# Which PSUM banks share a tile in the scan's paired column blocks, and how the planner of the order sees PSUM

## The chip, the cores and the metric

The kernel runs on one core of a Trainium2 chip. The metric is the time of one launch on the device, in microseconds (us), lower is better. A core has engines that work side by side, each with a queue of instructions of its own that it takes in order: TensorE (PE, matrix products into PSUM), VectorE (DVE), ScalarE (ACT), GpSimd (POOL), and SyncE (SP), whose queue here issues the loads and stores (DMAs). Engines wait for each other through semaphores. Products land in PSUM, in banks of 512 fp32 columns; the kernel's tiles there take eight banks.

## The reference

One layer of a streaming encoder for 512 prompt tokens and 64 sample tokens, which the kernel treats together as T = 576 columns. A combined input projection feeds a sparse attention (branch A) and a Mamba-2 scan (branch B); both are merged, and a SwiGLU FFN follows. The change lies in branch B, which in the reference is:

```python
full = jnp.concatenate([state_conv, xbc], axis=1)
xbc_c = jax.nn.silu(causal_conv(full, w_conv, b_conv, t))
xs, bm, cm = jnp.split(xbc_c, [D_INNER, D_INNER + SSM_GROUPS * D_STATE], axis=-1)
...
y, h_last = ssd_scan(xh, dtp, -jnp.exp(a_log), bm, cm, state_ssm, min(SSD_CHUNK, t))
y = (y + d_skip[:, None] * xh).reshape(b, t, D_INNER) * jax.nn.silu(z)
y = rms_normalize(y.reshape(b, t, SSM_GROUPS, -1)).reshape(b, t, D_INNER) * g_ssm_norm
```

xbc is a part of h @ w_in. It has 32 blocks of 128 channels: for each of the eight groups g two blocks of x (2g, 2g+1), one of B (16+g) and one of C (24+g). Each block is projected, convolved over four taps, and put through SiLU; then the scan goes over the tokens in chunks of 128 (and one of 64 for the sample stream).

## The kernel before

**Products.** Everything is fp32, and each matrix is kept as a high part and a low part in the type fp32r (names ending in h and l: hTh, hTl for the activations, wh, wl for a weight's two parts). A product is the sum of three matmul passes: high by high, high by low, low by high. The T columns are cut in halves of TH = 288.

**Pairs.** For groups 2 to 6 (PAIRED) the two x blocks are made together with Strassen's scheme, from seven products in place of eight. Product p takes an operand from the activations (A11, A12, A22, or one of the sums S1 to S4, kept in shS and slS) and one from the weights. Each product is 12 matmuls of 128x288: four slices, three passes. pair_split prepares the seven weights in four steps, two at a time: the first of a step goes to a tile of tag wh, the second to one of tag wl, and here each of these tiles holds a weight's high and low part both. So in the profile products 1, 6, 5, 3 appear with wh and 7, 2, 4 with wl; 1, 2, 4 with hTh and hTl, and 7, 6, 5, 3 with shS and slS.

Three banks collect them (PAIR): x takes 1, 6, 5, 3 one upon the other, z takes 7 and 4, y takes 2. After each product its bank is evicted into xc, the input of the convolution: by ScalarE copies after 1, 7, 6 and 3, and by VectorE adds after 2, 5 and 4 (LANDS). A half that holds sample columns is evicted in two pieces, 224 and 64 wide. Then the bank goes on: the next product adds to what stands in it. stage_a(g, 2) issues products 1, 7, 6, 2, and stage_a(g, 3) issues 5, 4, 3 and the two convolutions (conv_out).

**PSUM tiles.** pmm makes a tile of two banks (tag mm, two slots taken in turn), px a tile of one (tags px and py, two slots each). pair_begin takes two tiles of tag mm: y is in the first bank of one, x and z are the two banks of the other. Groups 0, 1 and 7, and every B and C block, use fm instead: one mm tile, each half of the columns in a bank. So a paired group takes four mm slots: B, C, and the pair's two.

**The convolution** (conv_out) of one block is: a small copy of the state (cvo), ScalarE's u = w3 * xc + bias (cu), three VectorE steps that add the other taps (cu), ScalarE's tanh (cth), and two VectorE steps that form SiLU into xb.

**The scan.** stage_b(g, c) does chunk c of group g: decay matrices on POOL and ScalarE (dec), transposes of x and B by TensorE, weighted copies (xdt, xw, bt, cs), the state (hst), and the products of y. In the loop over g, stage_b(g, i) is followed by stage_a(g+1, i) for i = 0 to 3, so the projections of the next group fill TensorE while a group is scanned. Every second group stage_c normalises two groups.

**The planner.** build() doesn't emit instructions at once. Each call makes an Op in a Plan; order() then simulates the engines with estimated costs (cost) and picks, per engine, the ready operation with the lowest prio (the running number, less an offset: R.prio(4000) puts an operation ahead of 4000 earlier ones). emit() issues the operations in the planned order, all from one line, which is why every row of the profile says L545. What depends on what is found by _touch from the boxes of the views (View.box): for PSUM, box() gives the 512-wide banks that a view covers. The semaphores themselves aren't set by the planner: the layer below adds them, from the accesses to each tile in the order in which they are emitted.

**Weight splits.** fetch() loads weights in queue order and split() makes their two parts: ScalarE copies the high part; the low part is a VectorE subtraction, or, for queue items 27 to 47, a second ScalarE pass and an accumulating DMA issued by POOL. Items 27 and 28 are the last two blocks of the filler work behind the attention's first key head.

Of the kernel before, what the change touches and what calls it, by code (L numbers as in the profile page):

```python
# [13 lines left out]
P = 128  # L14
D = 1024
NP_, NS = 512, 64
T = NP_ + NS
TH = T // 2
# [14 lines left out]
class View:  # L33
# [91 lines left out]
    def box(self):  # L125
        b = self.base
        if b.kind == "psum":
            f0 = self.off % b.pitch
            last = f0 + sum((n - 1) * s for n, s in self.dims[1:])
            return (0, P, f0 // 512 * 512, last // 512 * 512 + 512)  # L130
        if b.kind == "dram":
            last = self.off + sum((n - 1) * s for n, s in self.dims)
            return (0, 1, self.off, last + 1)
        p0, f0 = divmod(self.off, b.pitch)
        last = f0 + sum((n - 1) * s for n, s in self.dims[1:])
        return (p0, p0 + self.dims[0][0], f0, last + 1)
# [113 lines left out]
class Plan:  # L250
# [92 lines left out]
    def cost(self, op, outs, ins):  # L343
        e, fn = op.eng, op.fn
        o = outs[0] if outs else None
        if e == "sync":
            v = o if o is not None else ins[0]
            n = 4
            for k in v.shape:
                n *= k  # L350
            op.bytes = n
            row = 4 * v.shape[-1]
            op.rate = 300e3 if row >= 4096 else 345e3 if row >= 1024 else 250e3 if row >= 512 else 225e3
            return 0.06, 0.93
        if fn == "dma_start" and e == "scalar":
            op.bytes = 4 * _cols(ins[0]) * ins[0].shape[0]
            return 0.45, 0.93
        n = _cols(o)
        if e == "tensor":
            op.mm = True  # L360
            if fn == "transpose":
                return 0.110, 0.10
            rhs = op.args[2]
            fast = rhs.dtype == F32R
            n = _cols(rhs)
            if fast:
                return (n / 2.25 + 4 if n > 128 else 110) / 1e3, 0.10
            if op.kw.get("tile_position") is not None:
                return (73 if o.shape[0] <= 32 else 132) / 1e3, 0.10
            return ((4 * max(n, 128) / 2.4 if n > 1 else 190) + 5) / 1e3, 0.10  # L370
        if fn == "dma_start":
            op.bytes = 4 * n * o.shape[0]
            return 0.9, 0.93
        psum = any(is_psum(v) for v in ins)
        if e == "scalar":
            t = n / 1.2 + (52 if psum else 92) + (96 if isinstance(op.kw.get("bias"), View) else 0)
            return (t + (93 if op.kw.get("accum_out") is not None else 0)) / 1e3, 0.19
        if e == "vector":
            if fn == "tensor_reduce":
                n = _cols(ins[0])  # L380
            if fn in ("max", "match_replace"):
                n = _cols(ins[0] if fn == "max" else o)
            if fn == "reciprocal":
                return (69 + 6.25 * n) / 1e3, 0.13
            src = sum(1 for v in ins if _cols(v) > 1)
            fast = src == 1 and fn in ("tensor_copy", "tensor_scalar") and not is_psum(o) and not psum
            column = fn in ("scalar_tensor_tensor", "tensor_scalar") and len(ins) > src
            more = 60 * column + 70 * (fn == "tensor_tensor_reduce")
            return (64 + 0.96 * more + n * (0.5 if fast else 1.0)) / 0.96e3, 0.13
        if fn == "memset":  # L390
            return (n * 0.5 + 60) / 1e3, 0.1
        if op.kw.get("op") == OP.pow or OP.pow in op.args:
            return (n * 165 + 300) / 1e3, 0.1
        per = {"tensor_copy": 3.33, "affine_select": 1.0, "tensor_tensor": 2.1}[fn]
        return (n * per + 150) / 1e3, 0.1
# [157 lines left out]
def build(tc, I, O):  # L553
    R = Plan(tc)
# [3 lines left out]
    psum = R.mkpool("ps", space=PSUM)  # L558
# [5 lines left out]
    def pmm(name):  # L564
        return psum.tile([P, 2, 512], F32, name=name, tag="mm", bufs=2)
# [23 lines left out]
    def load_raw(src, nk, n):  # L589
        raw = wp.tile([P, nk, n], F32, name=f"raw{cnt[0]}", tag="raw", bufs=NRAW)  # L590
        sync.dma_start(raw, src)
        return raw
# [25 lines left out]
    raws, outs, outs_made = {}, {}, []  # L618
# [51 lines left out]
    def fetch(done, limit=1 << 30):  # L670

        while len(outs_made) < len(specs):
            i = len(outs_made)
            outs_made.append(i)
            queue.extend((i, s) for s in specs[i])
            outs[i] = []
        with R.prio(4000 if done else 0):
            more = True
            while more:
                more = False  # L680
                j = state["ld"]
                need = 0
                if j < min(len(queue), limit):
                    need = 1 if queue[j][1][0] != "pair" else 0 if queue[j][1][3] else 2
                if j < min(len(queue), limit) and raw_open[0] + need <= NRAW and j < state["sp"] + 4:
                    i, s = queue[j]
                    raw_open[0] += need
                    if s[0] == "pair":
                        w, c0 = s[1:3]
                        if need:  # L690
                            g, u = (load_raw(kview(w[:, c0 + P * a:c0 + P * a + P]), 8, P) for a in range(2))
                            pair_raw[c0] = {"B11": g[:, 0:4], "B21": g[:, 4:8], "B12": u[:, 0:4], "B22": u[:, 4:8]}
                        raws[j] = (c0, s[3])
                    elif s == "misc":
                        raw = wp.tile([P, 8, 104], F32, name="rawm", tag="raw", bufs=NRAW)
                        sync.dma_start(raw[:, :, 0:72], kview(w_in[:, C_KI:C_KI + 72]))
                        sync.dma_start(raw[:, :, 72:104], kview(w_in[:, C_DT:C_DT + 32]))
                        raws[j] = (raw, 8, 104)
                    else:
                        raws[j] = (load_raw(*s), s[1], s[2], 27 <= j < 48)  # L700
                    state["ld"] += 1
                    more = True
                j = state["sp"]
                if j < min(state["ld"], limit) and (j < NWH or queue[j - NWH][0] < done):
                    if queue[j][1][0] == "pair":
                        raw_open[0] -= 2 * (queue[j][1][3] == 3)
                        outs[queue[j][0]].append(pair_split(*raws.pop(j)))
                    else:
                        raw_open[0] -= 1
                        outs[queue[j][0]].append(split(*raws.pop(j)))  # L710
                    state["sp"] += 1
                    more = True
# [66 lines left out]
    for tb in range(5):  # L779
        n = P if tb < 4 else NS  # L780
        t = sp.tile([P, D], F32, name=f"xt{tb}")
# [125 lines left out]
    for tb in range(5):  # L907
        n = P if tb < 4 else NS
# [56 lines left out]
    with R.prio(-1500):  # L965
        for tb in range(5):
            n = P if tb < 4 else NS
# [23 lines left out]
    t = px("pwc")  # L991
# [76 lines left out]
    for i in range(2):  # L1068
        g = gqk[:, i, :]
# [120 lines left out]
    for hf in range(2):  # L1190
        x = ap_.tile([P, 5, 256], F32, name=f"qi{hf}", tag="tok", bufs=2)
# [69 lines left out]
    for b in range(5):  # L1261
        n = P * (b + 1) if b < 4 else T
# [3 lines left out]
    for b in (4, 1, 2, 3):  # L1266
        smp = b == 4
        n = T if smp else P * (b + 1)
# [200 lines left out]
    pair_now = {}  # L1469

    def pair_begin(g):
        py_, pxz = pmm(f"px{g}y"), pmm(f"px{g}x")
        pair_now[g] = {"y": py_[:, 0, :TH], "x": pxz[:, 0, :TH], "z": pxz[:, 1, :TH],
                       "xc": [conv_in(f"cv{g}_{i}", 2 * g + i - 2) for i in (2, 3)]}

    def pair_product(g, p):
# [137 lines left out]
    def stage_a(g, i):  # L1614
        if i == 0:
            bcs[g] = sd.tile([P, 2, T + 3], F32, name=f"bcx{g}", tag="bcx", bufs=3)
        if i == 2:

            xbs[g] = sd.tile([P, 2 * T + P - NS], F32, name=f"xb{g}", tag="xb", bufs=3)
            pool.memset(xbs[g][:, 2 * T:], 0.0)  # L1620
        if i >= 2 and g in PAIRED:
            if i == 2:
                pair_begin(g)
            for p in ((1, 7, 6, 2), (5, 4, 3))[i - 2]:
                pair_product(g, p)
            if i == 3:
                for a in range(2):
                    conv_out(f"cv{g}_{2 + a}", 2 * g + a, pair_now[g]["xc"][a], xbs[g][:, a * T:(a + 1) * T])
                del pair_now[g]
            return  # L1630
        ft = (16 + g, 24 + g, 2 * g, 2 * g + 1)[i]
        dst = bcs[g][:, i, :] if i < 2 else xbs[g][:, (i - 2) * T:(i - 1) * T]
        conv(f"cv{g}_{i}", ft, fm(f"px{g}_{i}", getw(), hh, hl), dst)
# [796 lines left out]
```

## Time and profile before

| what | value |
|---|---|
| time, three runs | 1382.48 us median (1381.15 to 1383.5) |
| the profiled execution: its time | 1381.79 us |
| the profiled execution: its span | 1380.1 us |
| granted TensorE clock, mean | 0.998 |
| instructions | 27974 |
| ScalarE copies xc<-mm in the whole kernel | 96, 207 to 413 ns |
| VectorE adds xc<-xc,mm in the whole kernel | 20, 208 to 456 ns |
| VectorE convolution steps cu | 96, median 817 ns |

The span reaches from the first to the last instruction of one execution; the time of that execution is a little longer. A row of the timeline has start, duration, engine, line, operation, output<-inputs, shapes, a count, and in brackets how long the engine stood idle before it and which engine and tile ended that. The durations of matmuls overlap: each is listed with about 0.29 us, while the next of a stream starts 0.13 to 0.14 us after it. PEld is the weight load that goes with a matmul. A view of waits has waiting engine and tile, releasing engine and tile, then total us, times, and the longest. A view of groups has busy time and mean ns of one, then the idle time ahead of them and who ended it. Names are the program's with numbers left out: xc is any group's convolution input, mm any tile of that tag.

### The profile page before, as it was taken

The page shows a single profiled execution, that of the slowest core. Times are in us where ns is not written, and L with a number is a line of the kernel's source. Part 1 is how long each engine was busy: PE and PEld are TensorE (multiplying, and loading weights), DVE is VectorE, ACT ScalarE, POOL GpSimd, SP SyncE. Part 2 cuts the span into 40 slices and gives each one's busy share as a digit, 9 for nine tenths or more (in the row PEclk, how much of TensorE's full clock was granted, in tenths as well). Part 3 has the DMA queues.
Part 4 walks back from the last instruction along what each step waited for, and adds up shares of the span by engine and source line. Part 5 has one row for each costly group of instructions (what it writes and reads, how often), then busy time and mean ns, then how long its engine had stood idle before and what let it go on. Part 6 is the DMA issues. An engine that isn't in the chain of part 4 may idle for free.

```text
span 1380.1 us, 27974 instructions
## 1 busy us (share of the span) xinstructions
PE 1344.9 (97%) x10617; PEld 1301.1 (94%) x10617; DVE 1168.2 (85%) x2354; ACT 818.0 (59%) x1873; POOL 200.4 (15%) x254
## 2 busy tenths in 40 slices
PE   7999999999999999989999999999999999999998
PEld 6999999999999888888889999999999999999998
DVE  5788999786778798888889769887799999888897
ACT  5435344777776677867878553124576666666453
POOL 2212003230300111322323320001100000000000
PEclk9999999999999999999999999999999999999999
DMA  9772436573853434333475578778623343325352
GB/s 300 218 191 68 118 111 160 115 177 95 193 150 88 121 94 112 101 111 97 134 214 148 196 231 272 239 213 251 187 63 108 93 130 100 92 71 156 96 158 65
DMA packets 268454, 201.36 MB, mean 146 GB/s; under 512 B 25552, under 2 KB 239680, under 8 KB 268320
## 3 DMA queue, kind: packets, MB, share of 16 engines
q1 hardware_dynamic: 263056, 183.40, 45.2%
q0 software_dynamic: 4976, 16.05, 5.9%
q8 instruction: 83, 1.36, 0.4%
q14 instruction: 51, 0.42, 0.1%
q10 hardware_dynamic: 288, 0.13, 0.0%
HBM read 157.75 MB, written 28.96 MB: 135 GB/s over the span
## 4 chain that ended last, share of the span: by engine, by line
PE 78%; ACT 8%; DVE 5%; DMA 4%; issue 3%; POOL 1%; SPq 0%; DVEq 0%; POOLq 0%; ACTq 0%
PE mm L545 54%; PE py L545 14%; PE px L545 10%; DMA raw<-in_w_in 2%; DVE cu L545 1%; ACT wh L545 1%; DVE wl L545 1%; ACT dec L545 1%; ACT hst L545 1%; ACT xc L545 1%; ACT cu L545 1%; ACT wl L545 1%; DMA y_d<-xb 1%; POOL r L545 0%; DVE wh L545 0%
## 5 line engine op out<-in xcount | busy, mean ns | idle before, releaser
L545 ACT ACTIVATE wh<-raw 128x1024 fp32r<-128x1024 f32 (+3 forms) x144 | 136.2, 948 | 138.3 <-PE mm L545 95.1
L545 PE MATMUL mm<-hTh,wl 128*128 128x288 f32 (+1 forms) x944 | 214.4, 303 | 2.6 <-ACT xc L545 1.9
L545 PE MATMUL mm<-hTh,wh 128*128 128x288 f32 (+1 forms) x904 | 205.0, 302 | 0.6 <-ACT wh L545 0.5
L545 PE MATMUL mm<-hTl,wh 128*128 128x288 f32 (+1 forms) x884 | 200.5, 302 | 0.9 <-DVE hTl L545 0.9
L545 PEld LDWEIGHTS mm<-hTh,wl 128*128 128x128 f32 (+1 forms) x944 | 154.1, 189 | 5.4 <-ACT xc L545 2.6
L545 PEld LDWEIGHTS mm<-hTh,wh 128*128 128x128 f32 (+1 forms) x904 | 147.6, 189 | 3.2 <-ACT hTh L545 0.8
L545 PEld LDWEIGHTS mm<-hTl,wh 128*128 128x128 f32 (+1 forms) x884 | 144.8, 189 | 3.2 <-DVE hTl L545 1.4
L545 DVE TENSOR_TENSOR wl<-raw,wh 128x1024 fp32r<-128x1024 f32 (+2 forms) x89 | 110.9, 1249 | 13.9 <-ACT wh L545 13.5
L545 POOL DMA_DIRECT2D wl<-raw x24 | 21.3, 889 | 468.6 <-PE px L545 313.8
L545 DVE SCALAR_TENSOR_TENSOR cu<-xc,wc,cu 128x579 f32<-128x579 f32 x96 | 80.0, 846 | 0.6 <-ACT cu L545 0.4
L545 PE MATMUL mm<-wh,hTl 128*128 128x256 f32 x256 | 72.5, 284 | 0.0
L545 PE MATMUL mm<-wl,hTh 128*128 128x256 f32 x256 | 72.3, 283 | 0.0
L545 PE MATMUL mm<-wh,hTh 128*128 128x256 f32 x256 | 72.2, 284 | 0.0
L545 DVE SCALAR_TENSOR_TENSOR aacc<-adr,sil,aacc 128x512 f32<-128x512 f32 x84 | 58.4, 748 | 6.3 <-DMA adr<-in_w_ada 6.2
L545 PE MATMUL mm<-shS,wh 128*128 128x288 f32 x248 | 55.0, 308 | 3.8 <-ACT xc L545 2.2
L545 PE MATMUL mm<-yh,wl 128*128 128x288 f32 x256 | 55.1, 296 | 0.0
L545 PE MATMUL mm<-xhS,wh 128*128 128x290 f32 (+1 forms) x248 | 54.8, 296 | 0.0
L545 PE MATMUL mm<-yh,wh 128*128 128x288 f32 x256 | 54.6, 295 | 0.0
L545 PE MATMUL mm<-yl,wh 128*128 128x288 f32 x256 | 54.6, 294 | 0.0
L545 ACT ACTIVATE P<-lg,mn 128x128 f32<-128x128 f32 (+4 forms) x72 | 41.7, 581 | 19.2 <-DVE mn L545 18.3
L545 PE MATMUL mm<-xhS,wl 128*128 128x290 f32 (+1 forms) x232 | 51.2, 296 | 0.0
L545 POOL TENSOR_TENSOR cs<-bc,bcx 128x512 f32<-128x512 f32 (+1 forms) x32 | 43.2, 1350 | 51.8 <-ACT bc L545 28.2
(612 smaller groups left out, 4278.4 us busy)
## 6 DMA issues: line engine op xcount, KB each, us to landing
raw<-in_w_in SPq DMA_DIRECT2D x80, 512.0 KB, 4.0
adr<-in_w_ada SPq DMA_DIRECT2D x36, 512.0 KB, 5.5
raw<-in_w_gate_up SPq DMA_DIRECT2D x22, 512.0 KB, 3.8
wl<-raw POOLq DMA_DIRECT2D x21, 512.0 KB, 5.3
rawu<-in_w_gate_up SPq DMA_DIRECT2D x20, 512.0 KB, 3.9
bc<-acs_d SPq DMA_DIRECT2D x32, 256.0 KB, 3.9
raw<-in_w_branch_ssm SPq DMA_DIRECT2D x16, 512.0 KB, 5.1
gate_d<-sg SPq DMA_DIRECT2D x16, 288.0 KB, 2.2
```

The costliest lines, as they stand in the source:

```text
L545: getattr(engines[x.eng], x.fn)(*[real(a) for a in x.args], **{k: real(v) for k, v in x.kw.items()})
```

## The change

Five edits:

1. pair_begin: x is in a tile alone, and y and z are the two banks of the other; the tile of x is taken first.
2. View.box: a view of PSUM covers its whole tile, whichever bank it lies in.
3. stage_a: the operations of the pairs' convolutions get the offset 600.
4. cost: for ScalarE, 96 ns are added for a scale that is a view, as they were for a bias.
5. fetch: the low parts of queue items 27 and 28 are made by VectorE; the range by DMA starts at 29.

```diff
     def box(self):
         b = self.base
         if b.kind == "psum":
-            f0 = self.off % b.pitch
-            last = f0 + sum((n - 1) * s for n, s in self.dims[1:])
-            return (0, P, f0 // 512 * 512, last // 512 * 512 + 512)
+            return (0, P, 0, b.free)
...
         if e == "scalar":
-            t = n / 1.2 + (52 if psum else 92) + (96 if isinstance(op.kw.get("bias"), View) else 0)
+            t = n / 1.2 + (52 if psum else 92) + 96 * sum(isinstance(op.kw.get(a), View) for a in ("bias", "scale"))
...
-                        raws[j] = (load_raw(*s), s[1], s[2], 27 <= j < 48)
+                        raws[j] = (load_raw(*s), s[1], s[2], 29 <= j < 48)
...
     def pair_begin(g):
-        py_, pxz = pmm(f"px{g}y"), pmm(f"px{g}x")
-        pair_now[g] = {"y": py_[:, 0, :TH], "x": pxz[:, 0, :TH], "z": pxz[:, 1, :TH],
+        px_, pyz = pmm(f"px{g}x"), pmm(f"px{g}y")
+        pair_now[g] = {"x": px_[:, 0, :TH], "y": pyz[:, 0, :TH], "z": pyz[:, 1, :TH],
                        "xc": [conv_in(f"cv{g}_{i}", 2 * g + i - 2) for i in (2, 3)]}
...
             if i == 3:
                 for a in range(2):
-                    conv_out(f"cv{g}_{2 + a}", 2 * g + a, pair_now[g]["xc"][a], xbs[g][:, a * T:(a + 1) * T])
+                    with R.prio(600):
+                        conv_out(f"cv{g}_{2 + a}", 2 * g + a, pair_now[g]["xc"][a], xbs[g][:, a * T:(a + 1) * T])
                 del pair_now[g]
```

## The prediction

> **What bounds the kernel now.** I read the page first, then the table of stretches, then TensorE's waits in the stretch of the paired groups, and last the timeline around single waits.
>
> ```profile
> span 1380.1 us, 27974 instructions
> ...
> PE 1344.9 (97%) x10617; PEld 1301.1 (94%) x10617; DVE 1168.2 (85%) x2354; ACT 818.0 (59%) x1873; POOL 200.4 (15%) x254
> ```
>
> TensorE (PE) is busy for 97% of the span, so only PE time that goes away shortens the kernel. It stands still for 1380.1 - 1344.9 = 35.2 us; the question is how much of that belongs to this change. The table of stretches (columns: stretch, length, then busy time and count of PE, PEld, DVE, ACT, POOL):
>
> ```profile
> 140.00:320.00 180.00, 179.16 (x1341) 175.16 (x1339) 160.38 (x401) 96.88 (x188) 32.05 (x27) 1.00 0.53 135
> 320.00:455.00 135.00, 134.12 (x985) 128.90 (x984) 99.61 (x263) 95.00 (x210) 19.04 (x33) 1.00 0.52 128
> 480.00:510.00 30.00, 26.49 (x211) 24.83 (x211) 28.04 (x51) 21.51 (x67) 6.00 (x7) 0.94 0.31 82
> 970.00:1245.00 275.00, 275.00 (x2075) 273.78 (x2074) 251.62 (x464) 178.32 (x357) 3.53 (x4) 1.00 0.36 105
> ```
>
> The paired groups (2 to 6) run their seven products between 510 and 710 us. The same table, taken there in five stretches of 40 us, ends with this row:
>
> ```profile
> sum 200.00, PE 184.06 PEld 171.14 DVE 169.07 ACT 145.80 POOL 53.89; mean PE 36.81 PEld 34.23 DVE 33.81 ACT 29.16 POOL 10.78
> ```
>
> PE idles 0.84 us in 140 to 320, 0.88 in 320 to 455, nothing in 970 to 1245, but 15.9 of 200 us here. The view of waits, PE alone, 510 to 710 us (total, times, longest):
>
> ```profile
> PE mm L545 <- ACT xc L545: 7.6, 13, 1.4
> PE mm L545 <- DVE xc L545: 3.9, 7, 0.6
> PE px L545 <- POOL r L545: 2.2, 2, 1.6
> PE px L545 <- DVE dec L545: 1.4, 1, 1.4
> ```
>
> Twenty waits, 11.5 us, are for xc: the evictions of the product banks (ACTIVATE copies or VectorE adds into xc). That is four for each of five groups. The timeline of group 3 shows what one of them is:
>
> ```profile
> 573.28 0.30 PE L545 MATMUL mm<-hTh,wh 128*128 128x288 f32 x1
> ...
> 573.41 0.30 PE L545 MATMUL mm<-shS,wl 128*128 128x288 f32 x1
> ...
> 573.55 0.29 PE L545 MATMUL mm<-slS,wl 128*128 128x288 f32 x1
> 573.88 0.36 ACT L545 ACTIVATE xc<-mm 128x224 f32<-128x224 f32 x1
> ...
> 574.29 0.53 PE L545 MATMUL mm<-shS,wl 128*128 128x288 f32 x2 [0.45 <-ACT xc L545]
> 574.85 0.22 ACT L545 ACTIVATE xc<-mm 128x64 f32<-128x64 f32 x1 [0.62 <-PE mm L545]
> ...
> 575.13 0.19 PEld L545 LDWEIGHTS mm<-slS,wl 128*128 128x128 f32 x1 [0.55 <-ACT xc L545]
> 575.13 0.40 PE L545 MATMUL mm<-slS,wl 128*128 128x288 f32 x1 [0.31 <-ACT xc L545]
> ```
>
> hTh with wh is product 1, in bank x; shS with the second weight (tile wl) is product 7, in bank z. The reader is to see that product 7 stops **in its own middle**, after its second matmul, until ScalarE has copied product 1 out of another bank; ScalarE's second piece then waits 0.62 us for product 7's matmuls in turn. Neither needs the other's data. The only thing that they share is the tile of two banks (x and z). So waits are set for the whole tile, while the planner, whose box() tells bank from bank, took z as free and put two matmuls ahead of the copy. Products 1, 7, 6 and later 5, 4, 3 all lie in this one tile: the ping-pong comes twice in the first half (7 behind 1, 6 behind 7) and twice in the second (4 and 3 behind the adds), the four found.
>
> A page speaks against this reading. The Trainium skill, "PSUM — Partial Sum Buffer", section "PSUM bank collisions raise a hardware error", has engines kept apart by bank and quadrant, and says that different banks run side by side; by that rule z needn't wait for x's reader, box() before was right, and taking a tile as one would only remove freedom. The row at 574.29 decides: this kernel does wait across banks. What the rule would make of the time is the third rival.
>
> **The change, part by part.**
>
> *The waits that go.* In the new layout x (products 1, 6, 5, 3) has a tile alone and y, z (2; 7, 4) share one. In the order 1, 7, 6, 2, 5, 4, 3 neighbours then always lie in different tiles, so each eviction has a whole other product to hide behind. Matmuls of one product start 0.14 us apart (573.41, 573.55), so twelve take 1.6 us. An eviction takes 0.36 + 0.22 us by the rows; with its handover, from the end of product 1 at 573.58 to ScalarE's start at 573.88, that is 0.9. The waits seen are 7.6 + 3.9 = 11.5 us. The idle column starts only at the modelled end of the matmul before (0.29 us), while the next could have begun 0.14 after its start: 573.55 to 574.29 is 0.74 us, 0.60 more than the pace, for an idle of 0.45. That adds 0.15 to each of twenty: 3.0. **Term: -14.5 us.** Bounds: 0 if nothing goes, -14.5 if all does. The engines across the ping-pong lose the same time, so it isn't their backlog that keeps PE:
>
> ```profile
> L545 DVE SCALAR_TENSOR_TENSOR cu<-xc,wc,cu 128x579 f32<-128x579 f32 x55 | 45.4, 837 | 0.4 <-ACT cu L545 0.3
> ...
> L545 DVE SCALAR_TENSOR_TENSOR xb<-cth,cu 128x512 f32<-128x512 f32 (+1 forms) x20 | 8.7, 462 | 1.2 <-ACT bt L545 1.2
> ...
> L545 DVE TENSOR_TENSOR xc<-xc,mm 128x288 f32<-128x288 f32 (+2 forms) x20 | 7.2, 377 | 9.8 <-PE mm L545 9.1 <-ACT xc L545 0.7
> ```
>
> DVE, in 510 to 710, idles 9.8 us ahead of its twenty adds.
>
> *The wait that comes.* The two slots of the mm tag are taken in turn: B, C, then the pair's two tiles, then the next B and C. Before, next B took y's slot, free since product 2; now it takes x's slot, which product 3, the last, holds until it is evicted. Group 4's end shows the price:
>
> ```profile
> 630.92 0.30 PE L545 MATMUL mm<-shS,wh 128*128 128x288 f32 x1
> ...
> 631.06 0.43 PE L545 MATMUL mm<-hTh,wh 128*128 128x288 f32 x2
> ...
> 631.26 0.47 ACT L545 ACTIVATE xc<-mm 128x224 f32<-128x224 f32 x2 [1.18 <-PE mm L545]
> ```
>
> B began at 631.06 beside the eviction; it would now begin after 631.73, 0.7 us later, 3.5 us for five groups. Next C (in the tile of y and z, free one product earlier) or the chunk's products can stand in, and so can win all of it back. Bounds 0 and +3.5 (7 if the copy is as late as the longest wait above, 1.4). In return the pair's first product, whose slot was C's, now gets B's and needn't wait for C's eviction. I take **+1.5**. Queued behind a waiting B are only PE's own products, so the loss isn't passed on to ScalarE or VectorE at once.
>
> *What is late next.* If PE gets 14.5 of 200 us back, DVE's 169.07 us stand in 185.5: 91%. Elsewhere DVE bore 160.38 of 180 (89%) with PE idling 0.84, and 251.62 of 275 (91.5%) with no idle. So this share alone needn't bind, but this stage has chains through DVE (dec, xw, the state) that the other two lack. If 89% is its limit, the stretch shrinks to 190, giving 4.5 us back. Bounds 0 and +4.5; I take **+2**, a bit under the middle, since the 91.5% row is the nearer one in load.
>
> *Convolution steps of pairs first (prio 600).* No instruction is added. The six cu steps and four xb steps of a pair's two blocks are 6 x 0.837 + 4 x 0.462 = 6.9 us of DVE a group, now placed ahead of chunk steps emitted up to 600 operations before. Cover: the next B and C, 96 matmuls, 13 us of PE. With it, nothing; a chunk that gets xb sooner could win part of 1.4 us (the wait for dec); without it up to 6.9 a group is lost (the fourth rival). I take 0.
>
> *Two weight splits (queue items 27, 28) by VectorE.*
>
> ```profile
> L545 DVE TENSOR_TENSOR wl<-raw,wh 128x1024 fp32r<-128x1024 f32 (+2 forms) x89 | 110.9, 1249 | 13.9 <-ACT wh L545 13.5
> L545 POOL DMA_DIRECT2D wl<-raw x24 | 21.3, 889 | 468.6 <-PE px L545 313.8
> ```
>
> Two POOL issues of 0.9 us, their accumulating DMAs and two ScalarE passes go; two DVE subtractions of 1.25 us come, during the attention's first filler groups. DVE has 99.61 of 135 us there and PE idles 0.88: 0, with +2.5 if DVE were late and -0.9 if all that idle went.
>
> *The planner's prices and boxes.* An activation with a scale from SBUF costs 96 ns more in the plan, and mm tiles count as one everywhere. No instruction gets longer, but the whole program may be ordered anew. In 140 to 455 and 970 to 1245 PE idles 1.7 us in all, so little can be won; what can be lost I bound by the largest stretch outside the pairs, 480 to 510 (3.5 us idle), on either side. I take 0.
>
> **Sum:** -14.5 + 1.5 + 2 = -11 us. The profiled execution took 1381.79 us, so 1370.8; the median of the runs shown is 1382.48, 0.7 above it, so I forecast 1371.5.
>
> **The rivals.**
>
> 1. *All of it, and some more.* Next C covers B's wait, DVE bears 91%, and earlier convolutions take part of the waits for r and dec (3.6 us together). -14.5 to -18: 1364 to 1368. For it: the FFN's Strassen pairs (970 to 1245), which have x, y and z in tiles of their own, show PE without idle. Against: fewer chains there.
> 2. *VectorE becomes the bound.* It keeps its time and the stretch stops at 89 to 87% DVE: 190 to 194 us, plus the +1.5: 1376 to 1380. For it: DVE 28.04 of 30 us with 3.5 us PE idle in 480 to 510. Against: the 9.8 us that DVE itself idles at the banks.
> 3. *The change doesn't do what it says,* because bank and tile are the same to the wait: then the waits are true ones (6 behind 1 in x), each bank keeps its products, and the time stays: 1380 to 1384. The stop inside product 7 is against it; that x must still be evicted before each reuse is for it.
> 4. *Slower: convolutions first starve the scan.* 6.9 us of DVE stand ahead of a chunk's dec, xw and state, and PE runs out of B and C. Up to 6.9 x 5 = 34 us; it decides from 11 / 5 = 2.2 us a group that aren't covered. At 4 us a group: +20 - 11 = +9, 1391. For it: PE waits for dec and xw today already. Against: 13 us of PE cover a group.
>
> **How the numbers follow.** The forecast (gain 7 to 14.5, 1368 to 1375.5) has 0.52; rival 1 0.16; rival 2 0.12; rival 3 0.10; rival 4 0.10. A measurement of this kernel tells about 0.2% (2.8 us) from no change: faster 0.52 + 0.16 + 0.12 = 0.80, same 0.10, slower 0.10. The range 1364 to 1381 holds the forecast, rival 2, most of rival 1 and a part of rival 3: 0.8.
>
> **What would show it.** Right: in the pairs PE's waits for xc fall from 20 to a handful, products run 1, 7, 6, 2, 5, 4, 3 in unbroken twelves, DVE's idle ahead of its adds falls from 9.8 to under 4 us, PE's idle between 510 and 710 from 15.9 to about 5. The second term shows as waits of B (hTh with wh) for xc, at most five. Rival 2 shows as PE waiting for dec, xw or bt instead; rival 4 as the same with long cu runs ahead of them. What would make it wrong: xc waits that stay at four a group, or a stage outside the pairs that gets idle through the new order.

## The result and the profile after

The changed kernel takes 1371.12 us (median of 6 runs, 1369.2 to 1373.5) against 1382.76 (6 runs): ratio 0.9917, 95% interval [0.9904, 0.9931], or 11.6 us less. The forecast was 1371.5. The profiled execution took 1369.76 us. The head of its page:

```profile
span 1368.0 us, 27974 instructions
...
PE 1343.4 (98%) x10617; PEld 1302.3 (95%) x10617; DVE 1170.2 (86%) x2356; ACT 815.3 (60%) x1871; POOL 199.1 (15%) x252
```

The reader is to see that PE has the same 10617 matmuls and 1.5 us less of busy time; what went is idle time, 1368.0 - 1343.4 = 24.6 us against 35.2. PE's waits in the pairs' stretch, now 500 to 705 us:

```profile
PE py L543 <- DVE xwS L543: 1.9, 1, 1.9
PE py L543 <- ACT bt L543: 1.1, 2, 0.9
PE px L543 <- DVE dec L543: 0.5, 2, 0.3
PE mm L543 <- ACT xc L543: 0.5, 1, 0.5
...
PE mm L543 <- ACT hst L543: 0.2, 1, 0.2
```

Of twenty waits for xc and 11.5 us, one of 0.5 us is left. The timeline of one pair in the changed kernel, at the place where product 7 stood still before:

```profile
605.30 0.30 PE L543 MATMUL mm<-hTh,wh 128*128 128x288 f32 x1
605.44 0.30 PE L543 MATMUL mm<-shS,wl 128*128 128x288 f32 x1
...
605.57 0.30 PE L543 MATMUL mm<-slS,wl 128*128 128x288 f32 x1
605.71 0.43 PE L543 MATMUL mm<-shS,wl 128*128 128x288 f32 x2
...
605.80 0.44 ACT L543 ACTIVATE xc<-mm 128x224 f32<-128x224 f32 x2
...
605.98 0.30 PE L543 MATMUL mm<-slS,wl 128*128 128x288 f32 x1
```

Product 7 follows product 1 at the usual 0.13 to 0.14 us, and runs on while ScalarE copies product 1 (605.80): the same two operations as at 573.88 and 574.29 before, without a stop. VectorE, in the view of groups of 500 to 705 us:

```profile
L543 DVE TENSOR_TENSOR xc<-xc,mm 128x288 f32<-128x288 f32 (+2 forms) x20 | 7.0, 372 | 0.8 <-PE mm L543 0.6
```

Its idle time ahead of the adds fell from 9.8 to 0.8 us. The row of the stretch of 200 us:

```profile
500.00:700.00 200.00, 195.27 (x1625) 185.88 (x1624) 180.82 (x339) 157.67 (x457) 55.25 (x71) 0.99 0.48 136
```

PE idles 4.7 us in it (15.9 before) and VectorE is busy for 90%. The two stretches are of one length but hold different amounts of work: 1625 matmuls here, 1495 before.

To say where in the span time went, I cut each profile at two marks that hold for all kernels: the first ScalarE copy xc<-mm (the scan's first eviction), and the first matmul of yh with wh (the merge). Their rows in the views by tile (after the durations stand first and last start). The kernel before, tile xc, then tile yh:

```profile
L545 ACT ACTIVATE xc<-mm x96: 207/352/413, 453.8 to 746.4; 128x288 f32<-128x288 f32 x32, 128x224 f32<-128x224 f32 x32, 128x64 f32<-128x64 f32 x32
```

```profile
L545 PE MATMUL mm<-yh,wh x256: 288/293/398, 829.2 to 933.9; 128*128 128x288 f32 x128
```

The changed kernel, the same two views:

```profile
L543 ACT ACTIVATE xc<-mm x96: 203/350/424, 455.0 to 722.7; 128x288 f32<-128x288 f32 x32, 128x224 f32<-128x224 f32 x32, 128x64 f32<-128x64 f32 x32
```

```profile
L543 PE MATMUL mm<-yh,wh x256: 288/293/406, 816.1 to 921.8; 128*128 128x288 f32 x128
```

The scan, from mark to mark, took 375.4 us and takes 361.1: 14.3 less. Ahead of it 1.2 us were lost (453.8 to 455.0), behind it 1.0 (550.9 to 551.9); both are less than the 2 us by which the first mark moves at one and the same order, as the next section shows. The evictions alone now last 267.7 us from first to last, not 292.6: the projections end 25 us sooner, and 11 of these come back behind them. Most of that is work and not idling. From the last eviction to the merge PE now has 796 matmuls in 93.4 us, against 707 in 82.8 before; chunk products that stood among the projections now follow them. PE idles 2.6 us of these 93.4, against 0.4 before.

### The profile page after: what moved, and what is told of

It reads as the page before. It is cut to its first block, busy times and chain, and to the rows that moved or that the text cites. A ratio compares the mean times of both kernels' runs of the same rounds, so it can differ in the third digit from the quotient of the medians.

```text
span 1368.0 us, 27974 instructions
## 1 busy us (share of the span) xinstructions
PE 1343.4 (98%) x10617; PEld 1302.3 (95%) x10617; DVE 1170.2 (86%) x2356; ACT 815.3 (60%) x1871; POOL 199.1 (15%) x252
## 4 chain that ended last, share of the span: by engine, by line
PE 73%; DVE 9%; ACT 6%; DMA 5%; issue 3%; SPq 2%; POOL 1%; POOLq 0%; DVEq 0%; ACTq 0%
PE mm L543 50%; PE py L543 13%; PE px L543 10%; DMA raw<-in_w_in 2%; SPq L543 2%; DVE cu L543 2%; ACT dec L543 1%; DVE wl L543 1%; DMA bc<-acs_d 1%; ACT wh L543 1%; DVE xb L543 1%; DMA wl<-raw 1%; ACT hst L543 1%; DMA yl<-y_d 0%; POOL dec L543 0%
## 5 line engine op out<-in xcount | busy, mean ns | idle before, releaser
L543 PE MATMUL mm<-hTh,wl 128*128 128x288 f32 (+1 forms) x944 | 217.3, 304 | 0.0
L543 ACT ACTIVATE dec<-dec,dtp 128x128 f32<-128x128 f32 x128 | 42.8, 395 | 15.8 <-POOL dec L543 13.2
```

Of the source, the lines that this page charges most:

```text
L543: getattr(engines[x.eng], x.fn)(*[real(a) for a in x.args], **{k: real(v) for k, v in x.kw.items()})
```

## The experiments

Twelve kernels, in three batches; each was timed against the kernel before on the same chip (medians of before 1383.28, 1383.38 and 1383.04). In the table, "ahead" is the time of the first mark, "scan" the time between the two, both from the one profiled execution; "xc" is PE's waits for xc (times, us; only waits that the view lists). How far the first mark moves by itself can be seen where the order up to it is the same, instruction by instruction on every engine. There are three such sets: before and e1_layout (453.8 both); the changed kernel, e4_no_prio, e15_no_layout and e16_same_order (455.0, 457.0, 456.9, 456.9); e2_box and e3_layout_box (463.1, 463.7). So one order moves by up to 2 us, and the kernels of one set are a single draw of the order ahead of the scan.

Two things blur the table. The mark cuts off slightly different work: PE has 3541 matmuls ahead of it in most kernels, but 3552 in e2_box, e3_layout_box and e9_price90 and 3526 in e6_no_price, that is 1.5 us more and 2.0 us less. And a few waits for xc stand ahead of the pairs, at 461 to 475 us: one of 1.5 us each in e2_box and e3_layout_box, two of 2.6 us together in e9_price90.

| kernel | label | median us | ratio to before | ahead | scan | xc |
|---|---|---|---|---|---|---|
| before | | 1382.76 | | 453.8 | 375.4 | 20, 11.5 |
| changed | | 1371.12 | 0.9917 [0.9904, 0.9931] | 455.0 | 361.1 | 1, 0.5 |
| layout alone | e1_layout | 1370.16 | 0.9904 [0.9885, 0.9922] | 453.8 | 361.5 | 3, 1.5 |
| boxes alone | e2_box | 1390.03 | 1.0049 [1.0033, 1.0065] | 463.1 | 372.4 | 10, 8.2 |
| layout, boxes | e3_layout_box | 1380.50 | 0.9979 [0.9966, 0.9992] | 463.7 | 365.3 | 3, 2.2 |
| changed, no offset | e4_no_prio | 1370.00 | 0.9906 [0.9888, 0.9924] | 457.0 | 360.4 | 0 |
| changed, no price | e6_no_price | 1380.40 | 0.9979 [0.9968, 0.9990] | 457.5 | 370.6 | 5, 4.0 |
| changed, old splits | e7_no_split | 1367.25 | 0.9878 [0.9862, 0.9893] | 453.2 | 359.6 | 1, 0.5 |
| changed, 90 ns | e9_price90 | 1377.05 | 0.9956 [0.9942, 0.9969] | 460.1 | 363.3 | 4, 3.8 |
| changed, old boxes | e10_no_box | 1369.12 | 0.9895 [0.9882, 0.9909] | 452.3 | 363.0 | 2, 3.6 |
| same, 90 ns | e18_no_box_price90 | 1372.19 | 0.9917 [0.9900, 0.9935] | 452.0 | 363.5 | 1, 0.2 |
| layout, offset, price | e14_lay_price_prio | 1370.93 | 0.9910 [0.9892, 0.9928] | 452.5 | 362.8 | 2, 3.2 |
| changed, old layout | e15_no_layout | 1372.58 | 0.9922 [0.9905, 0.9940] | 456.9 | 362.7 | 4, 2.9 |
| changed, same order, z by x | e16_same_order | 1379.00 | 0.9967 [0.9954, 0.9980] | 456.9 | 369.0 | 21, 9.9 |

### Layout alone, boxes alone, both

My theory was that waits are set for a whole tile, so that the layout itself takes neighbours apart; the rivals, that waits go by bank (then nothing happens), or that the planner's new boxes do the work.

Layout alone is edit 1 on the kernel before:

```diff
-        py_, pxz = pmm(f"px{g}y"), pmm(f"px{g}x")
-        pair_now[g] = {"y": py_[:, 0, :TH], "x": pxz[:, 0, :TH], "z": pxz[:, 1, :TH],
+        px_, pyz = pmm(f"px{g}x"), pmm(f"px{g}y")
+        pair_now[g] = {"x": px_[:, 0, :TH], "y": pyz[:, 0, :TH], "z": pyz[:, 1, :TH],
```

> The kernel before with the new layout of the pair's banks alone; the planner still tells bank from bank. Mine (waits are set for the whole tile, so the layout itself takes the neighbours apart): PE's waits for xc fall from 20 to 8 or fewer and from 11.5 to 4 us or less; what is left is the planner's, since it takes y and z as free of each other; time 1373 to 1378. Rival A (waits are set for the bank): still about 20 waits, 1380 to 1384. Rival B (the planner's boxes do the work, the layout only goes with them): waits about 15 to 20, since the plan is still blind to them, 1379 to 1384.

Boxes alone is edit 2 on the kernel before:

```diff
-            f0 = self.off % b.pitch
-            last = f0 + sum((n - 1) * s for n, s in self.dims[1:])
-            return (0, P, f0 // 512 * 512, last // 512 * 512 + 512)
+            return (0, P, 0, b.free)
```

> The kernel before with the planner's boxes of whole tiles alone; x and z still share a tile. Mine: the waits stay in the chip's rules but the planner now sees them and puts chunk products into them: waits for xc 6 to 14, 3 to 7 us in total, none in the middle of a product that starts before the copy; time 1375 to 1380. Rival A (waits by the bank): the plan holds back what needn't wait, 1383 to 1388. Rival B (the boxes do the work): 1369 to 1373, waits under 3 us.

Both together:

> Layout and boxes together, without the offset of the convolutions, the price of the scale and the two splits. Mine (these two are the change): waits for xc under 1.5 us, 1369 to 1374, within 0.2% of the changed kernel. Rival (the convolutions' offset carries a part, since the next group's chunk waits for xb): 1374 to 1378, and PE waits for dec, xw or bt in the stretch of the pairs over 5 us where the changed kernel has 3.5.

The layout alone gave all of the gain, 1370.16 us, and more than I expected of it. PE's waits for xc in its profile:

```profile
PE mm L545 <- ACT xc L545: 1.0, 2, 0.5
...
PE mm L545 <- DVE xc L545: 0.5, 1, 0.5
```

Three in place of twenty, with a planner as blind as before: the rival of waits by the bank, which expected about twenty, falls, and the new boxes aren't needed. Up to 530 us, where the pairs begin, every engine's order is that of the kernel before; from there on the order is new too, so what the place does by itself is shown only by e16_same_order below. The boxes alone made the kernel slower, 1390.03. Of the forecasts only the rival of waits by the bank had more time, 1383 to 1388, and none had a loss ahead of the scan:

```profile
PE mm L543 <- ACT xc L543: 8.2, 10, 1.7
...
PE px L543 <- DVE dec L543: 4.5, 3, 2.1
...
PE mm L543 <- DMA wl<-raw: 1.6, 1, 1.6
```

In the scan they won 3.0 us (375.4 to 372.4); ahead of it they lost 9.3 (453.8 to 463.1), where the layout isn't touched at all. Both together kept that loss (463.7, the same order up to the pairs) and ended at 1380.5: my forecast of 1369 to 1374 was wrong, the rival's 1374 to 1378 too, and so was the idea that these two are the change. The wait for a DMA into wl pointed to the splits, the other new thing was the price: hence the next batch.

### Which of the small edits pays for the boxes

The offset was taken out first:

```diff
-                    with R.prio(600):
-                        conv_out(f"cv{g}_{2 + a}", 2 * g + a, pair_now[g]["xc"][a], xbs[g][:, a * T:(a + 1) * T])
+                    conv_out(f"cv{g}_{2 + a}", 2 * g + a, pair_now[g]["xc"][a], xbs[g][:, a * T:(a + 1) * T])
```

> The changed kernel without the offset of 600 for the pairs' convolutions alone. Mine (the offset is worth nothing, as I counted it): 1369 to 1374. Rival C (it is worth time): 1374 to 1378, with PE waits for dec, xw, bt. Rival D (it costs time: convolutions ahead of chunks push scan work behind the last projections, where PE idles 2.5 us in the changed kernel and 0.4 before): 1365 to 1369, and that idle gone.

1370.00, with an interval of the ratio that overlaps the changed kernel's: the offset is worth nothing that can be measured here. Then the price (edit 4) and the splits (edit 5), each undone in the changed kernel:

```diff
-            t = n / 1.2 + (52 if psum else 92) + 96 * sum(isinstance(op.kw.get(a), View) for a in ("bias", "scale"))
+            t = n / 1.2 + (52 if psum else 92) + (96 if isinstance(op.kw.get("bias"), View) else 0)
```

> The changed kernel without the planner's price for a scale. So far: the layout alone took 13 us off, boxes alone added 7, layout and boxes took 3, and the whole without the offset took 13: so the price or the two splits win back some 10 us that the boxes lose ahead of the scan (the scan's first eviction at 463 us in place of 454). Theory S (the splits do it: with whole-tile boxes PE waits for a low part made by DMA, 1.5 us near 253, and all behind is late): still 1369 to 1373, first eviction at 454 to 458. Theory P (the price does it): 1377 to 1383, first eviction at 461 or later.

```diff
-                        raws[j] = (load_raw(*s), s[1], s[2], 29 <= j < 48)
+                        raws[j] = (load_raw(*s), s[1], s[2], 27 <= j < 48)
```

> The changed kernel with items 27 and 28 split by DMA as before. Theory S: 1377 to 1383, PE waits for a DMA into wl near 250 again, first eviction of the scan at 461 or later. Theory P: 1369 to 1373 and first eviction at 454 to 458.

And a control, a price that means nothing:

```diff
-            t = n / 1.2 + (52 if psum else 92) + 96 * sum(isinstance(op.kw.get(a), View) for a in ("bias", "scale"))
+            t = n / 1.2 + (52 if psum else 92) + 90 * sum(isinstance(op.kw.get(a), View) for a in ("bias", "scale"))
```

> The changed kernel with 90 in place of 96 ns for a bias or a scale in the planner: a change without a meaning, to measure what a new order by itself moves. If the plan is steady: 1370 to 1373. If the order is a lottery (rival to S and P both: whatever touches the plan moves some us): 3 us or more away from 1371, with the first eviction of the scan moved by over 2 us.

Taken alone, the first two would say that the price is worth 9 us and the splits cost 4. The control forbids it: 6 ns in the planner, which change no instruction, moved the kernel from 1371.12 to 1377.05, with intervals of the ratio that don't touch, and its first mark by 5 us (455.0 to 460.1), as the rival of a lottery had it. An edit that sets a new order has to move more than that before it is credited with anything. The 4 us of the splits don't; the 9 us of the price do, but one control is one draw and sets no upper bound. Theory S falls: without the two splits by VectorE no wait for a DMA into wl came back, and the kernel is the fastest of all, below what either theory had forecast. Theory P's time came true for the price, but not its place: it named the part ahead of the scan (461 us or later), while that kernel has 457.5 there and loses 9.5 us in the scan (370.6, of which 2.0 are the matmuls that moved behind its mark), so it isn't shown either. What exactly the boxes do to the order ahead of the scan stays open.

### The boxes out, and two more draws

```diff
-            return (0, P, 0, b.free)
+            f0 = self.off % b.pitch
+            last = f0 + sum((n - 1) * s for n, s in self.dims[1:])
+            return (0, P, f0 // 512 * 512, last // 512 * 512 + 512)
```

> The changed kernel with the old boxes (planner tells bank from bank); layout, offset, price and splits stay. Mine (the layout is the gain, the boxes only cost): waits for xc under 3 us, first eviction of the scan at 453 to 456, 1366 to 1371. Rival (the boxes pay once price and splits are in): 1373 to 1378, with six or more waits for xc.

With 90 ns in place of 96 as in the control above, on this kernel:

> The kernel without the new boxes (layout, offset, price, splits), with 90 in place of 96 ns. With the new boxes the same 6 ns moved the time by 6 us. If plans with the new layout are steady as long as the old boxes stay: 1367 to 1371, within 2 us of the 1369.1 measured with 96. If the lottery of orders has nothing to do with the boxes: 3 us or more away, on either side.

And this kernel with the old range of splits (27 to 47):

> Layout, offset and price with the old boxes and the old range of splits: what the runs so far would pick, since boxes cost or did nothing and the kernel without the two splits was 4 us faster than the changed one. If these add up: 1364 to 1368. If each is only another draw of the order: 1367 to 1373.

1369.12, 1372.19 and 1370.93. The first time was as forecast, but its two waits for xc, 3.6 us, are more than the 3 us that I had allowed. The second missed the 1367 to 1371 of a steady plan and by 3.1 us goes, just, to its rival. With layout alone that makes four plans with the old boxes, 1369.1 to 1372.2, all with the first mark at 452.0 to 453.8. Six plans with the new layout and the new boxes (five orders ahead of the scan) lie between 1367.3 and 1380.5, with the first mark at 453.2 to 463.7. So the boxes aren't needed for the gain; with them orders scatter over 13 us, without over 3. That is four draws against six, a hint and no proof. The 6 ns gave 3.1 us here, half of what they gave with the new boxes, and the two intervals overlap. The last kernel didn't add up to the 1364 to 1368 that sums of single edits promised.

### The same order with the old neighbours

All of these also set a new order. To see the wait by itself I kept the changed kernel's order and moved only bank z, when the instructions are emitted, from y's tile to the second bank of x's:

```diff
+    @staticmethod
+    def z_by_x(v):
+        pair = getattr(v.base, "pair", None)
+        return View(pair, v.off, v.dims, v.chain) if pair is not None and v.off % v.base.pitch >= 512 else v
...
-        real = lambda a: a.real() if isinstance(a, View) else a
+        real = lambda a: self.z_by_x(a).real() if isinstance(a, View) else a
...
         px_, pyz = pmm(f"px{g}x"), pmm(f"px{g}y")
+        pyz.base.pair = px_.base
```

> The changed kernel with every engine's order kept exactly as it is; only bank z is moved at emission, from y's tile to the free second bank of x's tile, so x and z share a tile again. Mine (waits for a neighbour's eviction in the same tile are the loss, whatever the order): about 20 waits for xc again, 10 to 15 us in total, two of them inside product 7 or 4; 1382 to 1388. Rival A (waits go by bank): no wait more, 1370 to 1373. Rival L (the time is a matter of the order alone): 1370 to 1374.

Each engine has the same instructions in the same order; only the place of z differs. PE's waits, 490 to 700 us:

```profile
PE mm L548 <- ACT xc L548: 5.2, 12, 0.6
PE mm L548 <- DVE xc L548: 4.7, 9, 0.9
PE py L548 <- ACT btS L548: 0.3, 1, 0.3
PE px L548 <- DVE dec L548: 0.2, 1, 0.2
```

and the same place of the same pair as shown above for the changed kernel:

```profile
608.32 0.30 PE L548 MATMUL mm<-shS,wl 128*128 128x288 f32 x1
...
608.65 0.36 ACT L548 ACTIVATE xc<-mm 128x224 f32<-128x224 f32 x1
...
609.06 0.40 PE L548 MATMUL mm<-shS,wl 128*128 128x288 f32 x1 [0.45 <-ACT xc L548]
...
609.63 0.23 ACT L548 ACTIVATE xc<-mm 128x64 f32<-128x64 f32 x1 [0.62 <-PE mm L548]
...
609.90 0.53 PE L548 MATMUL mm<-shS,wl 128*128 128x288 f32 x2 [0.32 <-ACT xc L548]
```

The stop in the middle of product 7 is back, with the idle times of the kernel before (0.45, then 0.62 on ScalarE, then 0.3), and 21 waits. Product 7 writes one bank and ScalarE reads another: the tile alone makes the difference. The time is 1379.0, 7.9 us more than the changed kernel's median (the scan, 369.0 against 361.1, says the same). Both rivals, at 1370 to 1374, fall; my own 1382 to 1388 was too high. The waits came nearly as expected, but the time shows less than they add up to: 9.9 us of waits and 21 x 0.15 for restarting make 13. Part of it stood in for other waits. In the changed kernel PE waits 4.0 us in the pairs for other things (the rows at the top: xwS, bt, dec and smaller ones), here 0.5; a PE that comes later finds them done. That accounts for 3.5 of the 5 us.

Last, the old layout with all else of the change, so that the planner knows that x and z share a tile:

> The changed kernel with the old layout alone, planned anew: the planner knows that x and z share a tile. Mine: the false waits are still there, but as far as it can the plan puts other work into them: 8 to 12 waits for xc, 5 to 9 us, 1378 to 1386. Rival (boxes, price, offset and splits carry it without the layout): 1369 to 1374.

1372.58: this time the rival was right. Only 4 waits for xc are left (2.9 us): the plan puts chunk products between the neighbours (24 matmuls between products 7 and 6 at 577.7 us, for one), and the scan takes 362.7 us. So there are two ways past the wait, banks that keep apart what follows each other, or a plan that knows of it. Boxes alone weren't enough for the second (10 waits, 8.2 us, nine of them in the pairs); what the price, the offset and the splits each add to it wasn't taken apart.

## Why the prediction was right

**The waits that go: right in mechanism, in size partly by luck.** The step "waits are set for the whole tile" is shown by the kernel that moves z alone. The term of -14.5 us was put on the pairs, and the scan became 14.3 us shorter. At a fixed order, though, 21 such waits cost 7.9 us and not 13: the term took each wait as fully lost, while a part of them hid other waits. So the close agreement is partly the new order's doing; how much of the 14.3 us is, these runs don't tell.

The products of the changed kernel run 1, 7, 6, 2, 5, 4, 3, as forecast, if not always in unbroken twelves. The prediction took the same order for the kernel before, and there it is another. The tile of y was taken first there, so product 2 (hTh and hTl with wl) ran ahead of product 1 (hTh with wh), and 4 came right behind 6. Group 3, PE alone:

```profile
569.55 0.64 PE L545 MATMUL mm<-hTh,wl 128*128 128x288 f32 x3
570.03 0.29 PE L545 MATMUL mm<-hTl,wl 128*128 128x288 f32 x1
...
571.73 0.38 PE L545 MATMUL mm<-hTh,wh 128*128 128x288 f32 x1
...
582.00 0.29 PE L545 MATMUL mm<-shS,wh 128*128 128x288 f32 x1
582.13 0.29 PE L545 MATMUL mm<-hTh,wl 128*128 128x288 f32 x1
...
584.64 0.40 PE L545 MATMUL mm<-hTh,wl 128*128 128x288 f32 x1 [1.23 <-ACT xc L545]
```

So in this group the four waits are two inside product 7, one inside 6 and one inside 4 behind ScalarE's copy of 6, not those that the prediction names; and the twenty are 4, 4, 6, 4 and 2 by group, not four in each. The reading that tiles and not banks wait isn't touched by this.

**The wait that comes (+1.5): it didn't come.** One wait for xc in the whole kernel, 0.5 us, is all that there is, at 639.6 us before a matmul of shS with wh, so it isn't B's; other work stood in each time. The upper end of 3.5 was far. In two plans with the old boxes, e10_no_box and e14_lay_price_prio, PE does wait once for xc before a matmul of hTh with wh, 2.2 and 1.8 us.

**What is late next (+2): there, but not a loss against before.** The 4.0 us named above are of this kind, against 4.8 us of other waits between 510 and 710 before (r, dec and smaller ones). VectorE bears 90% where I had worked out 91, and isn't the bound.

**Convolutions first (0): right within the measurement.** 1370.00 without, 1371.12 with. Rival 4 didn't show.

**Splits (0): not to be told from the order's own scatter,** and I put them in the wrong place. POOL's first two issues into wl, items 27 and 28, stand at 222 and 229 us in the timeline before, ahead of the attention, not in it; there VectorE is at 89%, not 74. The kernel that leaves this edit out was 3.9 us faster.

**The planner (0 on either side of 3.5): the weakest step.** The sum was right to 0.6 us by luck: two losses that I put into the scan, 3.5 us, weren't there, and a loss outside it that I had put at nothing was, 2.2 us in the one profile. The four kernels with its order ahead of the scan have the first mark 1.2 to 3.2 us behind that of before, so a loss there is likely and its size is rough. That a plan with the new boxes can lose 9 to 10 us ahead of the scan, as the one order of e2_box and e3_layout_box did, was outside my bound: I had taken the little idle time there as all that an order could touch, and bounded the loss by a stretch of idle from elsewhere. The changed kernel is the third fastest of the six plans with the new layout and boxes, 3.3 us under their mean.

**The rivals.** Rival 1 came near in the scan (-14.3) and was paid back outside. Rivals 2 and 4 didn't show; rival 2's range doesn't follow from its own terms, for 190 to 194 us in place of 200, plus 1.5, give 1374 to 1378 and not 1376 to 1380. Rival 3 falls by the kernel that moves z: a wait by bank would have left the time as it was. The rule named with it, that of the Trainium skill, "PSUM — Partial Sum Buffer", section "PSUM bank collisions raise a hardware error", keeps engines apart by bank and quadrant. No run here tests this rule of the Trainium skill on the chip itself; that the waits come and go with the tile says that this kernel's waits are coarser than the rule asks for.

**A better kernel.** The changed kernel with the old range of splits takes 1367.25 us, ratio 0.9878 [0.9862, 0.9893], below the changed kernel's interval. It may be a lucky order: 6 ns elsewhere moved as much, and with the old boxes the same step gave 1370.93 after 1369.12. The kernel with the layout alone, 1370.16, has the gain by one edit; moving z at a fixed order is worth 7.9 us, and what the rest of its 13 us is wasn't taken apart.

## What to carry to other kernels

When an engine stops in the middle of a product for an eviction that it doesn't need, look at which tile the two share, and move banks so that what follows each other lies in different tiles; the layout adds no instruction (27974 in both kernels). Before a re-planned kernel is credited to an edit, measure an edit without meaning beside it: here 6 ns in a cost moved the time by 6 us, more than most edits seemed to. To tell a wait from an order, keep the order and change only the place.

## What the runs showed that I had not expected

A more exact model came with a worse plan: with whole-tile boxes, which is how the waits really fall, the kernel took 1390.03 in place of 1383.28 us, since the order ahead of the scan, which has no pair in it, came out 9.3 us longer. It is one draw, and its 6.8 us are little more than the control's 6, so whether the model or the draw did it isn't shown. And a wait that is taken away returns less than its length where other work is nearly late: 13 us of stops at a fixed order were 7.9 us of time.
